# Two edits to a scheduled decoder-layer kernel: the extra tokens' values are written into the tile of the second sweep's transposed keys, and the first norm's weight is spread over the partitions ahead of its bias

## Chip, cores and metric

The kernel runs on one core of one Trainium2 chip. The metric is device time in microseconds (us) of one launch. Matrix multiplications run on TensorE (PE in the profile; PEld is its weight load), elementwise work on VectorE (DVE), ScalarE (ACT) and GpSimd (POOL); SyncE (SP) issues all DMA transfers.

## What is computed

One layer of a hybrid decoder for 2048 prompt tokens, 16 meta tokens and 32 sample tokens of width 1024, all in float32. Every token is layer-normed and multiplied by one wide input projection. Half of the result feeds a chunkwise linear recurrence (mLSTM, 4 heads of 128, chunks of 128 tokens), the other half a sliding-window attention (8 query heads, 2 key/value heads, window 128, a learned sink per head). Both halves are gated, joined, projected, added to the residual and layer-normed again.

```python
hp = layer_norm(concat([meta, x_prompt]), ln0_g, ln0_b)
hs = layer_norm(x_sample, ln0_g, ln0_b)
mq, mk, mv, mo, mz, mi, mf, aq, ak, av, az = split_proj(hp @ w_in[l] + b_in[l])
h_m, (c1, n1, m1) = mlstm_prompt(*mlstm_inputs(mq, mk, mv, mi, mf))   # chunk after chunk
h_a = swa_prompt(q_a, k_a, v_a, sink)                                  # banded blocks of 128
hp = layer_norm(DN_ALPHA * hp + concat([gate(h_m), gate(h_a)]) @ w_out, ln_g, ln_b)
```

The sample tokens go through the same layer with their own states and key/value caches. Outputs are both token sets, the states and the updated caches.

## The kernel before

The 2048 prompt tokens are 16 chunks of 128. The kernel goes over them twice. The **first sweep** (`a_steps`, to about 590 us) norms a chunk, projects q, k, v and the output gate of the recurrence, and runs the recurrence. The **second sweep** (`b_load` to `o_last`) does attention, gates, the output projection and the last norm. In the first sweep a generator `jobs` is advanced between the steps of the chunks; it does the 48 extra tokens' work (32 sample and 16 meta tokens), prepares the second sweep's weights and stores them.

Weights are split into two float16 parts (`prep_steps`: L259 and L261 find the largest value, L135 to L137 spread a maximum over the partitions by a product with an identity, L273 and L276 write the two parts). A product of a chunk with a weight of 512 columns is then 24 matmuls of 128x512 (L298, L299, L301). Chunk 0 doesn't wait for that: its four projections and the gates are taken from the raw float32 weights (`proj32`, L417). All projections write to two PSUM buffers of tag `pj`, so the third projection in a row needs the first one's result to have been copied out.

**The start.** The first norm's weight `gbr[:, 0:1024]` and bias `gbr[:, 1024:2048]` lie on one partition. Four matmuls with a row of ones spread them over 128 partitions: the bias at L359 into two `pt` buffers, which ACT copies to `bs` (L360); the weight at L369 into two `pj` buffers, which DVE reads directly for chunk 0 (L372, `(x - mean) * weight`, in two halves) and which ACT copies to `gs` (L375) for later chunks. L373 then multiplies by the reciprocal deviation and adds the bias. PE transposes the normed chunk (L450), ACT copies the transposes out (L451), and with that the first projection (L417) can start.

**The extra tokens' values.** `ve` is where the projected values of the 48 extra tokens stand, with a column of ones per head: 4 heads of 129 columns. It is `vaug[1]`. `vaug[0]` and `vaug[1]` are also where the values of even and odd chunks go (L430), and their columns of ones are set once. L317 writes `ve`; a DMA stores it to DRAM (`e_d`), and four small matmuls (L651) make the recurrence's first state `Cst[0]` from its meta tokens' rows. Chunk 1's values (L430) overwrite the same tile, so they stand behind both. The other extra tokens' results go the same way: L317 writes, `e_d` stores, and the first step of `d_head` (L690 and on) loads one head's part back into the tile `da`, from which PE transposes it (L699).

**What sets the order.** The text of the program is not the order of the instructions. The framework's scheduler replays the program with a cost table of its own and places each engine's instructions one by one; engines then run their lists strictly in that order and wait on semaphores. An edit in one place can therefore move instructions on all engines. Two orders are tied by hand: the first loads (`first`), and later transfers behind the load of a chunk (`Order.anchor`).

`kTs` holds the second sweep's transposed keys, 4 x 272 float16 per partition. Nothing reads or writes it in the first sweep until the meta tokens' keys are copied in (L888).

```python
ve = vaug[1][:NE]                                                     # L546
V.scalar_tensor_tensor(out, ps3, w.ev[:rows], t3, op0=ALU.mult, op1=ALU.add)   # L317, out = ve
c.v = vaug[n % 2]                                                     # L429
T.matmul(ps[:, i, :129], kwe[NS:NE, h], ve[NS:NE, h], start=True, stop=True)   # L651
```

Of the kernel before, what the change touches and what calls it, by code (L numbers as in the profile page):

```python
# [8 lines left out]
F32 = mybir.dt.float32  # L9
F16 = mybir.dt.float16  # L10
BF16 = mybir.dt.bfloat16
I32 = mybir.dt.int32
AF = mybir.ActivationFunctionType
# [3 lines left out]
P = 128  # L17
D = 1024
# [4 lines left out]
NE = NS + NM  # L23
H = 4
# [13 lines left out]
NW = 272  # L38
# [3 lines left out]
def tile_hymba_step(  # L42
# [7 lines left out]
    V, A, G, T, S = nc.vector, nc.scalar, nc.gpsimd, nc.tensor, nc.sync  # L50

    cst = ctx.enter_context(tc.tile_pool(name="cst", bufs=1))
# [6 lines left out]
    def psum(tag, shape, bufs):  # L59
        return pp.tile(shape, F32, tag=tag, name=tag, bufs=bufs)  # L60

    def pj():
        return psum("pj", [P, 512], 2)

    def pt(shape):
        return psum("pt", shape, 3)
# [4 lines left out]
    def po(shape):  # L71
        return psum("po", shape, 2)
# [8 lines left out]
    def work(tag, shape, dt=F32, bufs=None):  # L81
        return mn.tile(shape, dt, tag=tag, name=tag, bufs=bufs or KB4.get(tag, 1))
# [72 lines left out]
    ones = cst.tile([P, P], F32, name="ones")  # L155
# [16 lines left out]
    gbr = mn.tile([P, 2048], F32, tag="wkv", name="gbr")[0:1]  # L172
# [43 lines left out]
    vaug = [cst.tile([P, H, 129], F32, name=f"vaug{i}") for i in range(2)]  # L216
# [113 lines left out]
    def layer_norm_stats(x, rows, eps, tag):  # L330

        st = small(f"st_{tag}", 12)[:rows]
        for i in range(2):
            V.bn_stats(st[:, 6 * i:6 * i + 6], x[:, 512 * i:512 * i + 512])
        mv = small(f"mv_{tag}", 2)[:rows]
        V.bn_aggr(mv, st)
        ve = small(f"ve_{tag}", 1)[:rows]
        V.tensor_scalar(ve, mv[:, 1:2], eps, None, op0=ALU.add)
        rs = small(f"rs_{tag}", 1)[:rows]
        G.tensor_tensor(rs, ve, mhalf[:rows, 0:1], op=ALU.pow)  # L340
        return mv, rs
# [12 lines left out]
    V.tensor_scalar(xnorm, xnorm, 32.0, None, op0=ALU.mult)  # L354
    gs, bs = work("gb", [P, D]), work("gb", [P, D])

    for i in range(2):
        ps = pt([P, 512])
        T.matmul(ps, ones[0:1, :], gbr[:, D + 512 * i:D + 512 * i + 512], start=True, stop=True)  # L359
        A.activation(bs[:, 512 * i:512 * i + 512], ps, AF.Copy)  # L360
    bqk = cst.tile([P, 2], F32, name="bqk")
    all_max(bqk, bq2)

    def ln0_first(x):

        mv, rs = layer_norm_stats(x, P, EPS, "a")
        pg = [pj() for _ in range(2)]
        for i in range(2):
            T.matmul(pg[i], ones[0:1, :], gbr[:, 512 * i:512 * i + 512], start=True, stop=True)  # L369
        for i in range(2):  # L370
            c = slice(512 * i, 512 * i + 512)
            V.scalar_tensor_tensor(x[:, c], x[:, c], mv[:, 0:1], pg[i], op0=ALU.subtract, op1=ALU.mult)  # L372
        last = V.scalar_tensor_tensor(x, x, rs, bs, op0=ALU.mult, op1=ALU.add)  # L373
        for i in range(2):
            A.activation(gs[:, 512 * i:512 * i + 512], pg[i], AF.Copy)  # L375
        return last.ins
# [42 lines left out]
    def a_proj(n, i, st=None):  # L419
# [11 lines left out]
        else:  # L431
# [10 lines left out]
            if i == 3:  # L442
                A.activation(t, t, AF.Tanh, scale=0.5)

    ln0_first(x0)
    xf = [work(t, [P, 4, P]) for t in ("wt", "SI")]
    for i in range(2):
        ps = pt([P, 4, P])
# [94 lines left out]
    qe = work("qs", [P, 512])[:NE]  # L543
    ke = work("At", [P, 512])[:NE]
    oe = work("g", [P, 512])[:NE]
    ve = vaug[1][:NE]  # L546

    sto = stage(512, "w")
    load(sto, w_a[3])
# [14 lines left out]
    ps = pt([P, 8, NE])  # L564
# [3 lines left out]
    ps = pt([P, 8])  # L568
# [78 lines left out]
    for j in range(2):  # L647
        ps = po([P, 2, 256])
        for i in range(2):
            h = 2 * j + i  # L650
# [186 lines left out]
    mg = col(4)  # L837
    dma(mg, m_g)
    wB = {}

    kTs = cst.tile([P, 4, NW], F16, name="kTs")

    Vm = [cst.tile([P, 2, 4, 64], F16, name=f"Vm{i}") for i in range(2)]

# [673 lines left out]
```

## Time and profile before

| what | us |
|---|---|
| median of 3 runs (lowest to highest) | 1062.38 (1060.8 to 1063.92) |
| the profiled execution | 1059.23 |
| its span from the first to the last instruction | 1057.4 |
| PE busy | 1026.1 (97%) |
| DVE busy | 728.7 (69%) |
| ACT busy | 441.3 (42%) |
| POOL busy | 247.6 (23%) |
| mean granted TensorE clock | 0.993 |

The profile is one execution. A row of the timeline gives start and length in us, engine, source line, operation, the tile written and the tiles read, and in brackets how long the engine had been idle and what ended that. A row of the waits gives who waited for whom, the total, the number of times and the longest. A row of the windows gives busy time per engine in a stretch, then the granted clock. A row's numbers are taken from this execution, so that sums are made against 1059.23 us, of which 1.83 us lie around the span.

### The profile page before, as it was taken

Reading aid. Unit: us, or ns where it says so; the run is one execution under the profiler, and the core shown is the slowest. Engines: PE = TensorE matmul, PEld = TensorE weight load, DVE = VectorE, ACT = ScalarE, POOL = GpSimd, SP = SyncE. Lnnn points to the kernel's source line nnn. Section 1 sums busy time; section 2 is a strip of 40 time slices with the busy share of each in tenths; the row PEclk is TensorE's granted clock in tenths of the full one; section 3 lists DMA queues with packets and bytes.
Section 4 is the critical chain, followed back from the end, with each engine's and each line's share of the span. In section 5 each row is a group of like instructions: output and inputs, shape, how many; then the busy total and the mean of one; then the engine's idle time right before and its main releaser. Section 6 shows DMA issues by size and latency. Waiting matters only on the chain.

```text
span 1057.4 us, 17650 instructions
## 1 busy us (share of the span) xinstructions
PE 1026.1 (97%) x6399; PEld 571.0 (54%) x6399; DVE 728.7 (69%) x2056; ACT 441.3 (42%) x1112; POOL 247.6 (23%) x270
## 2 busy tenths in 40 slices
PE   7998999999999999999999999999999999999996
PEld 3544666655556555555565555555555455555552
DVE  5996876767766887787557676656566566666674
ACT  5783333336244554552334334343334333343430
POOL 2101313211111001013111332233331233332322
PEclk9998999999999999999999999999999999999998
DMA  9946366464794775755866463555445555545452
GB/s 332 267 133 164 99 145 154 115 187 88 233 236 123 222 247 140 231 133 160 291 188 124 92 160 89 132 131 117 108 113 127 128 124 139 108 102 135 113 114 76
DMA packets 245809, 161.83 MB, mean 153 GB/s; under 512 B 207945, under 2 KB 220953, under 8 KB 244409
## 3 DMA queue, kind: packets, MB, share of 16 engines
q1 hardware_dynamic: 245722, 160.70, 58.3%
q8 instruction: 50, 0.82, 0.3%
q14 instruction: 37, 0.30, 0.1%
HBM read 68.22 MB, written 43.58 MB: 106 GB/s over the span
## 4 chain that ended last, share of the span: by engine, by line
PE 69%; DMA 11%; DVE 10%; ACT 6%; issue 3%; POOL 1%; SPq 1%; DVEq 0%; ACTq 0%
PE pj L1351 14%; PE pj L301 14%; PE pj L298 14%; PE pj L299 14%; DMA stg<-hl 3%; PE pt L1271 3%; PE po L1324 2%; DMA stg<-in_dram 1%; DMA xT<-hl 1%; DMA kT<-kh 1%; ACT w_o L259 1%; DMA wd_o<-w_o 1%; DVE w_o L276 1%; PE po L816 1%; PE po L817 1%
## 5 line engine op out<-in xcount | busy, mean ns | idle before, releaser
L301 PEld LDWEIGHTS <-xT 128*128 128x128 f16 x992 | 96.9, 98 | 98.2 <-issue 1.0
L299 PEld LDWEIGHTS <-xT 128*128 128x128 f16 x992 | 97.4, 98 | 96.7 <-issue 5.2
L298 PEld LDWEIGHTS <-xT 128*128 128x128 f16 x992 | 97.4, 98 | 94.1 <-issue 2.8
L1351 PEld LDWEIGHTS <-EE 128*128 128x128 f16 x720 | 70.3, 98 | 79.0
L1351 PE MATMUL pj<-wr_o,EE 128*128 128x512 f16 x360 | 82.3, 379 | 0.0
L1351 PE MATMUL pj<-w_o,EE 128*128 128x512 f16 x360 | 82.1, 379 | 0.0
L1278 ACT ACTIVATE SI<-SI,nb 128x272 f32<-128x272 f32 (+1 forms) x64 | 32.4, 507 | 66.0 <-DVE nb L1275 66.0
L298 PE MATMUL pj<-w_o,xT 128*128 128x512 f16 x120 | 46.9, 390 | 3.2 <-DVE vaug L430 3.2
L1278 ACT ACTIVATE g<-g,nb 128x272 f32<-128x272 f32 (+1 forms) x64 | 32.2, 503 | 42.4 <-DVE nb L1275 42.4
L1284 POOL TENSOR_TENSOR mhl<-SI,mhl 128x32 f16<-128x32 f32 x32 | 12.6, 395 | 157.6 <-ACT mhl L1283 157.6
L298 PE MATMUL pj<-wr_az,xT 128*128 128x512 f16 x128 | 48.5, 379 | 0.0
L299 PE MATMUL pj<-wr_z,xT 128*128 128x512 f16 x128 | 48.5, 379 | 0.0
L298 PE MATMUL pj<-wr_aq,xT 128*128 128x512 f16 x128 | 48.5, 379 | 0.0
L299 PE MATMUL pj<-wr_aq,xT 128*128 128x512 f16 x128 | 48.5, 379 | 0.0
L299 PE MATMUL pj<-wr_az,xT 128*128 128x512 f16 x128 | 48.5, 379 | 0.0
L298 PE MATMUL pj<-wr_z,xT 128*128 128x512 f16 x128 | 48.5, 379 | 0.0
L793 POOL TENSOR_TENSOR qs<-qs,SI 128x512 f32<-128x512 f32 x16 | 20.9, 1307 | 113.5 <-ACT SI L784 113.3
L299 PE MATMUL pj<-w_o,xT 128*128 128x512 f16 x120 | 46.7, 390 | 0.0
L1181 POOL TENSOR_TENSOR xs<-xs,gb 128x1024 f32<-128x1024 f32 (+1 forms) x16 | 42.8, 2674 | 15.4 <-DMA stg<-hl 9.3
L298 PE MATMUL pj<-w_v,xT 128*128 128x512 f16 x120 | 46.0, 383 | 0.0
L299 PE MATMUL pj<-w_v,xT 128*128 128x512 f16 x120 | 45.8, 382 | 0.0
L792 POOL TENSOR_TENSOR qs<-qT 128x512 f32<-128x512 f16 x16 | 20.2, 1260 | 109.2 <-DMA qT<-qh 58.9
(463 smaller groups left out, 2492.1 us busy)
## 6 DMA issues: line engine op xcount, KB each, us to landing
stg<-in_dram SPq DMA_DIRECT2D x28, 512.0 KB
xs<-in_dram SPq DMA_DIRECT2D x16, 512.0 KB
h_d<-xs SPq DMA_DIRECT2D x16, 512.0 KB
xT_d<-xT SPq DMA_DIRECT2D x16, 512.0 KB
xs<-h_d SPq DMA_DIRECT2D x16, 512.0 KB
xT<-xT_d SPq DMA_DIRECT2D x16, 512.0 KB
out_dram<-xs SPq DMA_DIRECT2D x15, 512.0 KB
hn_d<-g SPq DMA_DIRECT2D x16, 258.0 KB
```

Of the source, the lines that this page charges most:

```text
L259: A.activation(w.t[:, 2 * i:2 * i + 2, 0, :], s, AF.Abs, accum_out=mx4[:, i:i + 1])
L298: T.matmul(ps, xT[:, k, :], w.t[:, k, 0, :n], start=(k == 0), stop=False)
L299: T.matmul(ps, xT[:, k, :], w.t[:, k, 1, :n], start=False, stop=False)
L301: T.matmul(ps, xT[:, KT + k, :], w.t[:, k, 0, :n], start=False, stop=(k == KT - 1))
L792: G.tensor_tensor(c.qs, c.qT[:, 0], c.qT[:, 1], op=ALU.add)
L793: G.tensor_tensor(c.qs, c.qs, c.SI, op=ALU.mult)
L1181: G.tensor_tensor(z, z, lg[:rows], op=ALU.mult)
L1271: T.matmul(ps[:, lo:], c.qT[:, h], kTs[:, 2 * (h // 4) + x, lo:], start=(x == 0), stop=(x == 1))
L1278: A.activation(p[:, i, lo:], p[:, i, lo:], AF.Exp, bias=nb[:, h:h + 1], accum_out=sums[:, h:h + 1])
L1284: G.tensor_tensor(m[:, 1], p[:, :, 2 * P:], m[:, 0], op=ALU.subtract)
L1324: T.matmul(pso[:, h], l, r, start=False, stop=(i == len(last) - 1), skip_group_check=True)
L1351: T.matmul(ps, c.yT[:, a, :], w[:, k, t, :], start=(first and j == 0), stop=(last and j == len(mm) - 1))
```

## The change

```diff
@@ -354,10 +354,6 @@
     gs, bs = work("gb", [P, D]), work("gb", [P, D])
 
-    for i in range(2):
-        ps = pt([P, 512])
-        T.matmul(ps, ones[0:1, :], gbr[:, D + 512 * i:D + 512 * i + 512], start=True, stop=True)
-        A.activation(bs[:, 512 * i:512 * i + 512], ps, AF.Copy)
     bqk = cst.tile([P, 2], F32, name="bqk")
     all_max(bqk, bq2)
 
@@ -367,6 +363,10 @@
         pg = [pj() for _ in range(2)]
         for i in range(2):
             T.matmul(pg[i], ones[0:1, :], gbr[:, 512 * i:512 * i + 512], start=True, stop=True)
+        for i in range(2):
+            ps = pt([P, 512])
+            T.matmul(ps, ones[0:1, :], gbr[:, D + 512 * i:D + 512 * i + 512], start=True, stop=True)
+            A.activation(bs[:, 512 * i:512 * i + 512], ps, AF.Copy)
         for i in range(2):
             c = slice(512 * i, 512 * i + 512)
             V.scalar_tensor_tensor(x[:, c], x[:, c], mv[:, 0:1], pg[i], op0=ALU.subtract, op1=ALU.mult)
@@ -543,7 +543,11 @@
-    ve = vaug[1][:NE]
+
+    kTs = cst.tile([P, 4, NW], F16, name="kTs")
+
+    ve = kTs.rearrange("p c t -> p (c t)").bitcast(F32)[:NE, 0:H * 129].rearrange("p (h d) -> p h d", d=129)
+    G.memset(ve[:, :, P:P + 1], 1.0)
@@ -838,8 +842,6 @@
-    kTs = cst.tile([P, 4, NW], F16, name="kTs")
-
```

The first edit writes the two bias matmuls and their copies behind the two weight matmuls. The second puts `ve` into the memory of `kTs`, seen as float32 (516 of its 544 words), so that `vaug[1]` belongs to odd chunks alone; a small memset sets the four columns of ones. No arithmetic is added or removed but that memset. The new file has the weight's matmuls at L365, the bias's at L368 and its copies at L369. From the third hunk on, a line of the new file is that of the old plus 4, and from the fourth on plus 2.

The scheduler makes another order of the whole first sweep from it; in the second sweep the order is the same again, from about 590 us on. Three places follow.

On DVE at the start, before, L373 (the norm's last step; `xs` is chunk 0, `gb` the bias) stands close behind the second L372. L137 and L135 are the two ends of a maximum that is spread through PE:

```order
L372 SCALAR_TENSOR_TENSOR xs<-xs,mv_a,pj 128x512
L261 TENSOR_REDUCE mx_268<-stg 128x1
L261 TENSOR_REDUCE mx_414<-tg 128x1 x3
L372 SCALAR_TENSOR_TENSOR xs<-xs,mv_a,pj 128x512
L598 MEMSET ea 128x8
L261 TENSOR_REDUCE mx_414<-tg 128x1
L135 TENSOR_SCALAR dg<-cs,gb_187 128x128
L373 SCALAR_TENSOR_TENSOR xs<-xs,rs_a,gb 128x1024
L265 TENSOR_REDUCE mx<-mx_268 128x1
L265 TENSOR_REDUCE mx<-mx_414 128x1
L137 TENSOR_REDUCE gbx<-po 128x2
L135 TENSOR_SCALAR dg<-cs,gb_198 128x128
```

And now, the last rows up to L373:

```order
L353 TENSOR_TENSOR cols<-gbx 128x1
L122 TENSOR_SCALAR cols<-cols 128x1
L354 TENSOR_SCALAR cols<-cols 128x1
L124 TENSOR_SCALAR cols<-cols 128x1
L265 TENSOR_REDUCE mx<-mx_270 128x1
L126 TENSOR_SCALAR cols<-cols 128x1
L265 TENSOR_REDUCE mx<-mx_416 128x1
L135 TENSOR_SCALAR dg<-cs,gb_198 128x128
L261 TENSOR_REDUCE mx_490<-stage 128x1
L137 TENSOR_REDUCE bqk<-po 128x2
L135 TENSOR_SCALAR dg<-cs,mx 128x128
L373 SCALAR_TENSOR_TENSOR xs<-xs,rs_a,gb 128x1024
```

Both L372 now stand ahead of L261, and L373 stands behind two whole spread maxima (`gbx`, `bqk`) and one reduction of a weight. PE's list has the L136 matmuls of these maxima ahead of the transposes L450 in the same way.

On ACT at the start, before (`gb<-pt` is a half of the bias, `gb<-pj` one of the weight, `wt` and `SI` hold chunk 0's transposes):

```order
L360 ACTIVATE gb<-pt 128x512 x2
L259 ACTIVATE w_q,mx_268<-stg 128x2x512 x3
L375 ACTIVATE gb<-pj 128x512
L323 ACTIVATE hl,lns<-xs 48x1024
L375 ACTIVATE gb<-pj 128x512
L259 ACTIVATE w_k,mx_488<-stage 128x2x512
L324 ACTIVATE lns<-lns 48x1
L451 ACTIVATE wt<-pt 128x512
```

And now:

```order
L369 ACTIVATE gb<-pt 128x512
L375 ACTIVATE gb<-pj 128x512 x2
L259 ACTIVATE w_q,mx_270<-stg 128x2x512 x3
L323 ACTIVATE hl,lns<-xs 48x1024
L369 ACTIVATE gb<-pt 128x512
L259 ACTIVATE w_k,mx_490<-stage 128x2x512
L324 ACTIVATE lns<-lns 48x1
L259 ACTIVATE w_k,mx_490<-stage 128x2x512
L325 ACTIVATE hl,lns<-xs,lns 48x1024
L620 ACTIVATE hl<-xs,cols 128x1024
L326 ACTIVATE lns<-lns,cols 48x1
L451 ACTIVATE wt<-pt 128x512
```

The second half of the bias has moved behind four long instructions, and the copy of the transposes (L451) behind four more.

On DVE where chunk 1's values are copied out (L430, `vaug_125` is `vaug[1]`), before; `mx_1803<-stg` reads the freshly loaded k/v weight of the second sweep, `da` the sample tokens' states, and `g<-px` is the last of the extra tokens' four projections:

```order
L696 COPY da<-ea 128x8
L614 COPY ea<-pt 48x12
L644 TENSOR_SCALAR kw<-At,ea 48x128 x4
L696 COPY da<-ea 128x8
L261 TENSOR_REDUCE mx_1803<-stg 128x1 x2
L311 TENSOR_TENSOR g<-g,bias 48x512
L261 TENSOR_REDUCE mx_1803<-stg 128x1
L317 SCALAR_TENSOR_TENSOR g<-px,cols,g 48x512
L430 SCALAR_TENSOR_TENSOR vaug_125<-pj,cols,bias 128x4x128
```

And now:

```order
L700 COPY da<-ea 128x8
L317 SCALAR_TENSOR_TENSOR kTs<-px,cols,g 48x4x128
L700 COPY da<-ea 128x8
L518 SCALAR_TENSOR_TENSOR gts<-pt,cols,bg 128x8
L809 SCALAR_TENSOR_TENSOR At<-pt,cols,wt 128x512
L261 TENSOR_REDUCE mx_1804<-stg 128x1
L519 SCALAR_TENSOR_TENSOR gts<-pt,cols,gts 128x8
L261 TENSOR_REDUCE mx_1804<-stg 128x1 x2
L472 SCALAR_TENSOR_TENSOR ls<-gts 128x4
L484 COPY Gi_123<-gts 128x4
L430 SCALAR_TENSOR_TENSOR vaug_125<-pj,cols,bias 128x4x128
```

L430 stands behind the same loads' readers (L700, L261) as before; L317 of the last projection (`g<-px`) has moved behind it. On PE, chunk 1's output gate projection stood behind the gates' matmuls before (`pj_1099`; `pt_847` are the gates):

```order
L516 MATMUL pt_847<-w_g_413,xT_616 128x8
L298 LDWEIGHTS xT_616
L298 MATMUL pj_1099<-w_o_620,xT_616 128x512
L299 LDWEIGHTS xT_616
L299 MATMUL pj_1099<-w_o_620,xT_616 128x512
```

And now it stands behind chunk 0's eight matmuls of L820 and L821 (L816 and L817 of the old file), which stood after it:

```order
L820 MATMUL po_922<-vaug0_124,At_799 128x129
L821 MATMUL po_922<-Cst0_673,qs_773 128x129
L820 MATMUL po_929<-vaug0_124,At_799 128x129
L821 MATMUL po_929<-Cst0_673,qs_773 128x129
L820 MATMUL po_929<-vaug0_124,At_799 128x129
L821 MATMUL po_929<-Cst0_673,qs_773 128x129
L298 LDWEIGHTS xT_618
L298 MATMUL pj_1100<-w_o_622,xT_618 128x512
```

## Prediction, made before the changed kernel was run

> **What bounds the kernel now.** I began with the page's totals (busy time, share of the span, count) and the granted clock, a digit of tenths for each of 40 slices:
>
> ```profile
> span 1057.4 us, 17650 instructions
> PE 1026.1 (97%) x6399; PEld 571.0 (54%) x6399; DVE 728.7 (69%) x2056; ACT 441.3 (42%) x1112; POOL 247.6 (23%) x270
> PEclk9998999999999999999999999999999999999998
> ```
>
> PE is busy for 97% of the span, so the time is PE's work plus PE's waits. The edits add no matmul; they can only move waits and the stretches at a lower clock. The waits of PE, by what ended them (total, times, longest):
>
> ```profile
> PE pt L359 <- DVE dg L135: 6.3, 1, 6.3
> ...
> PE pj L298 <- DVE vaug L430: 3.2, 1, 3.2
> PE pt L749 <- DVE Gf L483: 2.9, 2, 1.7
> PE pt L513 <- ACT am L773: 1.8, 1, 1.8
> PE po L136 <- DVE dg L135: 1.1, 2, 0.7
> PE pt L612 <- ACT ea L607: 1.1, 1, 1.1
> ```
>
> The row to see is L298's: 3.2 us for `vaug`, the very tile that the second edit separates from the extra tokens. The first row is the load of the first operands and stays. Then the stretches (length, busy time and count of PE, PEld, DVE, ACT and POOL, granted clock, DMA share, GB/s):
>
> ```profile
> 20.00:70.00 50.00, 50.00 (x196) 24.24 (x195) 45.79 (x125) 40.06 (x68) 7.08 (x6) 1.00 0.86 251
> 89.40:96.20 6.80, 4.43 (x11) 1.57 (x11) 5.92 (x21) 2.77 (x8) 1.27 (x1) 0.50 0.44 68
> 95.00:590.00 495.00, 487.40 (x3040) 283.05 (x3039) 358.27 (x1045) 206.29 (x495) 89.82 (x88) 1.00 0.63 172
> 396.60:400.00 3.40, 3.40 (x10) 1.17 (x9) 3.30 (x8) 3.40 (x11) 1.54 (x1) 0.50 0.30 111
> ```
>
> From 20 to 70 us PE has no gap: whatever delays its start by a microsecond delays the end by one. After 3.2 us idle the clock stood at 0.50 from 89.4 to 96.2, and once more at 396.6.
>
> **The start.** Timeline of before, first PE, then DVE and ACT:
>
> ```profile
> 6.26 3.75 PE L359 MATMUL pt<-gbr,ones 1*128 1x512 f32 x4 [6.26 <-DVE dg L135]
> 9.80 3.62 PE L369 MATMUL pj<-gbr,ones 1*128 1x512 f32 x4
> 14.88 0.79 PE L136 MATMUL po<-dg,ones 128*128 128x128 f32 x2 [0.74 <-DVE dg L135]
> 16.08 1.97 PE L450 MATMUL pt<-cs,xs 128*128 128x128 f32 x8 [0.40 <-DVE xs L373]
> 19.43 4.45 PE L417 MATMUL pj<-stg,wt 128*128 128x512 f32 x8
> 23.72 3.60 PE L417 MATMUL pj<-stage,wt 128*128 128x512 f32 x8
> ...
> 13.81 0.74 DVE L372 SCALAR_TENSOR_TENSOR xs<-xs,mv_a,pj 128x512 f32<-128x512 f32 x1
> 14.55 0.28 DVE L135 TENSOR_SCALAR dg<-cs,gb 128x128 f32<-128x128 f32 x1
> 14.74 1.28 DVE L373 SCALAR_TENSOR_TENSOR xs<-xs,rs_a,gb 128x1024 f32<-128x1024 f32 x1
> 16.07 0.41 DVE L137 TENSOR_REDUCE gbx<-po 128x2 f32<-128x256 f32 x1
> 17.04 1.21 DVE L261 TENSOR_REDUCE mx<-stage 128x1 f32<-128x1024 f32 x1
> ...
> 10.04 0.60 ACT L360 ACTIVATE gb<-pt 128x512 f32<-128x512 f32 x1 [1.11 <-PE pt L359]
> 12.61 1.04 ACT L259 ACTIVATE w_q<-stg 128x1024 f16<-128x1024 f32 x1
> 14.13 1.05 ACT L323 ACTIVATE hl<-xs 48x1024 bf16<-48x1024 f32 x1
> 17.27 0.57 ACT L451 ACTIVATE wt<-pt 128x512 f32<-128x512 f32 x1
> 17.75 1.14 ACT L616 ACTIVATE hl<-xs,cols 128x1024 f16<-128x1024 f32 x1
> ```
>
> The four spreading matmuls change places at equal cost, 3.75 against 3.62 us; each half is out 1.7 to 1.9 us after the one before. The weight's are now out at about 8.2 and 9.9, the bias's at 11.7 and 13.4. So L372 can run some 3.5 us earlier, but the chunk's norm ends with L373, which needs the bias, and that now comes last.
>
> ACT: first bias half at 11.7, two weight copies to 13.4 (0.6 each), three L259 at 1.04 to 16.5, L323 to 17.6, the second bias half to 18.1. In before the second half was there at 10.6. L323 and the L259 read other data, so nothing lets the copy past them: ACT's list is strict.
>
> DVE: the second L372 is no longer what L373 stands behind; it stands behind two spread maxima, each a round trip to PE. From a first L135 at 13.8, a trip takes about 1.2 us until L137 can start (14.55 to 16.07 here with L373 between; 1.2 without); L137, the next L135, seven tiny rows (0.6 together), one L261 (1.2), the second L137 (0.4) and L135 end at about 18.4. Both paths meet at 18.1 to 18.4, so L373 starts at 18.4, not 14.74: 3.7 later. L450 follows at 19.7. L451 stands on ACT behind two L259, L325, L620 (1.14, the old L616) and L326 from 18.1 on, to about 22.7, while the transposes are there at about 21; so ACT, not PE, sets L417's start: 22.7 and L451's 0.6 make 23.3 against 19.43, **+3.9**. Two pairs of L136 that stood later now run in that hole: −0.46 (0.23 a pair at full clock, as 0.38 us with overlap in a full stretch). Net **+3.4**.
>
> The clock at the start: the first eight rows of L417 took 4.45 us, the next eight 3.60, so 0.85 us were lost because PE began at the low rate, and the spreading matmuls ran low too (L369's four rows of 512 columns took 3.62 us, as long as L417's second eight). With a longer hole ahead of L417, PE may run low for one more window of about 3.4 us (half of 89.4 to 96.2): half of that is the most, 1.7. The new hole's own waste counts already, so 0 to 1.5; I take **+0.9**, the amount seen.
>
> Here the Trainium skill (TensorE: Matmul & The Clock Gate, Part 1: The HAM clock gate) says that one busy window of about 3.4 us raises the clock and one idle window lowers it. The trace disagrees at this place: PE was busy from 6.26 to 13.4 and L417 still began slowly. By the page the first matmuls would lift the clock in either order; by it the term is 0 and the sum 0.9 lower.
>
> **Around 90 us.** Rows of PE, DVE, ACT and SP:
>
> ```profile
> 80.35 0.29 PE L612 MATMUL pt<-cs,ea 128*48 128x128 f32 x1 [1.10 <-ACT ea L607]
> 91.77 0.58 PE L298 MATMUL pj<-w_o,xT 128*128 128x512 f16 x1 [3.19 <-DVE vaug L430]
> 99.23 0.31 PE L699 MATMUL px<-cs,da 32*128 32x32 f32 x2
> 104.44 0.39 PE L817 MATMUL po<-Cst,qs 128*128 128x129 f32 x2
> 73.59 3.65 DVE L276 SCALAR_TENSOR_TENSOR w_o<-stage,cols,w_o 128x1024 f16<-128x1024 f32 x3
> 85.54 0.17 DVE L696 COPY da<-ea 128x8 f32<-128x8 f32 x1 [1.53 <-DMA da<-in_dram]
> 87.72 1.50 DVE L261 TENSOR_REDUCE mx<-stg 128x1 f32<-128x512 f32 x2 [2.00 <-DMA stg<-in_dram]
> 90.33 0.73 DVE L317 SCALAR_TENSOR_TENSOR g<-px,cols,g 48x512 f32<-48x512 f32 x1
> 90.99 0.73 DVE L430 SCALAR_TENSOR_TENSOR vaug<-pj,cols,bias 128x512 f32<-128x512 f32 x1
> 96.45 0.31 ACT L706 ACTIVATE da<-da 32x128 f32<-32x128 f32 x1 [1.23 <-DMA da<-e_d]
> ```
>
> L430 was late not because of L651's reading: DVE had no idle time before it. It stood behind rows that waited for transfers (1.53 and 2.00 us). These transfers are issued when the preparation of `w_o` ends (77.2), and L430 ends 14.5 us after that. The separate tile alone gives nothing; the new order must. There, that end comes at about 78.3 (1.1 us more of DVE's rows ahead of it, counted from the list), and L430, with L317 of `g` behind it, ends 13.4 after: 91.7. PE arrives at `w_o` at 88.6 + 3.4 + 0.9 − 1.4 (L612, below) + 1.8 (eight matmuls L820/L821 now ahead, 0.22 each: starts 104.21 and 104.44) = 93.3. So PE no longer waits, with 1.6 us to spare: **−3.2** and, for the slow stretch behind it (PE's 4.43 us of it would take half at full clock), **−2.2**. The eight moved matmuls cost nothing in sum.
>
> L612's gap (1.1 and 0.3 for its queue) is filled since its rows stand earlier on all engines: **−1.4**, at worst 0.
>
> New: `g` now stands behind L430, with one L261, L433, L438, L311 and its own L317 (0.7 each) and nine tiny rows of about 0.15 from there on, 4.7 in all: it ends at about 96.4. From its end (91.06) to the first reader of the reloaded `da` (96.45) it took 5.4, so `da` is there at 101.8, while PE reaches L703 (the old L699; behind 24 matmuls of `w_o` at 0.216 and some 1.9 us of small ones, 7.1 in all) at 100.4: **+1.4 to 1.6**, here 1.6.
>
> The rest of the first sweep is in a new order too; its waits (L749 2.9, L513 1.8, four small ones 1.4, and 1.7 for the slow stretch at 396.6) make 7.8. I see no side for it: 0, bounds −7.8 to +7.8. The memset on POOL (23% busy) and the `kTs` tile, unused until the sweep's end, cost nothing; if POOL were late, L430 no longer reads that column, only L655 does.
>
> **Sum:** 3.4 + 0.9 − 1.4 − 3.2 − 2.2 + 1.6 = **−0.9**: 1059.23 − 0.9 = 1058.3 for such an execution. The median of the runs lies 3.15 above the profiled time, so 1061.5 against 1062.38.
>
> **Rivals.** *Faster (A):* half of the 7.8 us of small waits go with the new order on top: −3.9 more, −4.8, 1057.6. For it: each hangs on one row's place (L749 on `Gf`). Against: new orders make new waits.
>
> *Slower (B):* PE still waits for `vaug` L430, because its place on DVE behind the same transfers is unchanged. If the preparation of `w_o` ends 1.6 us later than 78.3 (half of the start's delay handed on), the wait begins; 3.2 later again, all of it is there. Then 3.2 + 2.2 stay; the wait at L703 falls to 1.2: −0.9 + 5.4 − 0.4 = +4.1, 1066.4. DVE was busy for 45.8 of 50 us from 20 to 70, so it has little room to catch up; that speaks for it.
>
> *Clock (C):* the new wait at L703 costs a slow window as the 1.8 us wait at L513 did at 396.6: +1.7, 1063.2. The Trainium skill's rule of a whole idle window (same section) speaks against it; the row at 396.6, where 1.8 us sufficed, for it.
>
> *The edit does not do what it says:* as found, freeing the tile gives nothing by itself; that is B's ground.
>
> **How the numbers follow.** Forecast −0.9: 0.38; C: 0.10; A: 0.30; B: 0.22. A measurement of this kernel tells about 0.3%, 3.2 us, from no change, so faster is below 1059.2, slower above 1065.6: A 0.30, B 0.22, the rest 0.48. Range: A with 2 us more to B with 0.6 more, 1055.5 to 1067.0; the bounds of the reordered rest beyond that are left out. The likeliest case alone spans 1059.5 to 1063.5 (start's clock 0 to 1.5, L612's gap kept).
>
> **What would show it.** L373 at about 18.4 and L417 at 23.3; no row of L298 waiting for `vaug`, and the clock at 1.00 from 80 to 96; a wait of 1 to 2 us at L703 for `da`; L749 and L513 still waiting about 5 us together. A start of L417 below 20 or a wait of 3 us for L430 would make the sum wrong; equal steps and a time off by over 4 us would mean the rest of the first sweep decided.

## The result, and the profile after

The changed kernel is slower: 1070.44 us median of 3 runs (1069.25 to 1071.47) against 1062.38, ratio 1.0055 [1.0031, 1.008]. Timed again with 12 runs against 29 of before it took 1069.57 against 1064.25, 1.0050 [1.0032, 1.0068]. The forecast was 1061.5, range 1055.5 to 1067.0.

The head of the page after, with busy time, share and count per engine:

```profile
span 1068.6 us, 17656 instructions
PE 1029.2 (96%) x6399; PEld 572.2 (54%) x6399; DVE 729.5 (68%) x2056; ACT 441.5 (41%) x1112; POOL 251.9 (24%) x271
```

PE's busy time grew by 3.1 us of 11.2, at the same number of matmuls; the rest are gaps. The waits of PE, by what ended them (total, times, longest):

```profile
PE po L1326 <- DMA stg<-hl: 6.2, 7, 2.8
...
PE px L738 <- DVE ea L722: 3.0, 2, 1.9
...
PE po L655 <- DVE kTs L317: 1.8, 1, 1.8
...
PE px L703 <- DMA da<-e_d: 1.4, 1, 1.4
```

No row of L298 waits for `vaug` and none of L616 (the old L612) for ACT. In their place stand L655, which reads `ve` out of `kTs`, and L738, a step of the sample tokens. The stretches that the prediction showed, and one that is new:

```profile
20.00:70.00 50.00, 49.66 (x189) 25.26 (x189) 45.01 (x125) 39.22 (x68) 5.54 (x5) 1.00 0.87 239
89.40:96.20 6.80, 6.80 (x41) 4.12 (x39) 6.55 (x17) 2.92 (x8) 1.15 (x1) 1.00 0.45 107
182.90:186.30 3.40, 3.40 (x10) 1.22 (x8) 3.40 (x12) 0.46 (x2) 0.12 (x1) 0.50 0.47 124
```

The granted clock (the number behind POOL's busy time) is 1.00 where it was 0.50 from 89.4 to 96.2, and 0.50 at 182.9.

Single waits don't add up to the difference, so PE's loss is counted for every matmul: the time to the next matmul's start, less what a matmul of that shape takes at full clock (the 25% quantile of the shape in the profiles of before and after). The loss holds gaps and low clock together; only the time ahead of about 6 us and the tail lie outside it. Two single runs far off, 1531 us of e1 and 2758 us of e6, are in no ratio. By stretch of the span, in us, with all runs (a ratio is the estimate on record, with its 95% interval, against before's runs on the same chip, and differs from the ratio of the two medians by up to 0.0011; "before" is the profile of the prediction):

| kernel | ratio [95%] | span | L417 starts | 0–40 | 40–70 | 70–130 | 130–240 | 240–480 | 480–600 | 600– |
|---|---|---|---|---|---|---|---|---|---|---|
| before | 1 | 1057.4 | 19.43 | 6.0 | 0.3 | 9.6 | 5.8 | 11.7 | 4.5 | 4.0 |
| b0_before | a single run | 1065.9 | 19.86 | 7.7 | 0.5 | 10.0 | 5.6 | 13.2 | 9.3 | 4.2 |
| f3_before_10 | 0.9976 [0.9956, 0.9996] | 1058.4 | 19.14 | 5.3 | 0.3 | 9.3 | 5.5 | 12.1 | 6.6 | 4.4 |
| after | 1.0055 [1.0031, 1.008] | 1068.6 | 23.04 | 10.0 | 0.2 | 5.5 | 10.7 | 12.1 | 6.7 | 7.8 |
| a0_after | 1.0050 [1.0032, 1.0068] | 1070.7 | 22.57 | 9.6 | 0.2 | 6.3 | 12.5 | 10.9 | 7.9 | 8.2 |
| f1_after_10 | 1.0031 [1.001, 1.0052] | 1061.0 | 22.28 | 10.6 | 0.2 | 5.0 | 8.4 | 12.3 | 4.7 | 5.4 |
| f2_after_24 | 1.0071 [1.0043, 1.0098] | 1070.9 | 22.13 | 9.7 | 0.3 | 5.5 | 10.6 | 15.0 | 6.7 | 8.9 |
| e1_bias_only | 1.0047 [1.0028, 1.0066] | 1070.8 | 22.89 | 9.6 | 0.2 | 6.8 | 8.9 | 12.1 | 9.5 | 8.3 |
| e2_ve_only | 1.0075 [1.0051, 1.0099] | 1071.5 | 19.20 | 7.0 | 0.5 | 10.1 | 6.6 | 17.3 | 6.5 | 8.8 |
| e4_tie | 1.0028 [1.0007, 1.0049] | 1065.5 | 22.71 | 10.5 | 0.2 | 6.4 | 7.0 | 13.2 | 5.2 | 7.9 |
| e6_decay8 | 1.0015 [0.9996, 1.0034] | 1062.9 | 23.22 | 9.0 | 0.2 | 6.1 | 5.7 | 11.6 | 7.0 | 7.5 |
| e5_start | 1.0101 [1.0077, 1.0126] | 1074.7 | 20.81 | 9.8 | 0.5 | 11.6 | 7.2 | 19.8 | 3.9 | 7.4 |
| e7_kv_behind | 1.0094 [1.0067, 1.0121] | 1071.8 | 19.26 | 7.0 | 0.5 | 11.9 | 7.8 | 18.2 | 5.8 | 5.8 |
| e8_short_start | 1.0134 [1.0099, 1.017] | 1073.9 | 18.74 | 8.0 | 1.1 | 14.8 | 9.2 | 11.1 | 5.8 | 9.2 |
| e9_both | 1.0129 [1.0098, 1.016] | 1075.5 | 19.23 | 7.7 | 1.5 | 18.4 | 6.5 | 11.1 | 6.3 | 8.8 |
| e10_final_dve | 0.9959 [0.9936, 0.9982] | 1053.8 | 19.81 | 6.9 | 0.4 | 9.5 | 6.3 | 9.8 | 1.9 | 4.2 |
| e11_o_dve | 0.9968 [0.9947, 0.9989] | 1057.7 | 19.53 | 6.2 | 0.5 | 9.4 | 5.6 | 13.2 | 1.4 | 5.8 |

The means of after, a0 and e1 (the same lists but for two swaps on DVE), less those of before and b0: +2.9, −0.2, −3.6, +5.0, −0.8, +1.1, +4.0, in all +8.4, as much as the mean spans differ. The ratio of the runs, 1.0050 of 1064.25, gives +5.3: a profile is one execution, and with 1.83 us around the span before's two lie 0.8 below their median, the other three some 2 above theirs.

### The profile page after: what moved, and what is told of

Its sections match the earlier page's. It is cut to its first block, busy times and chain, and to the rows that moved or that the text cites. A ratio compares the mean times of both kernels' runs of the same rounds, so it can differ in the third digit from the quotient of the medians.

```text
span 1068.6 us, 17656 instructions
## 1 busy us (share of the span) xinstructions
PE 1029.2 (96%) x6399; PEld 572.2 (54%) x6399; DVE 729.5 (68%) x2056; ACT 441.5 (41%) x1112; POOL 251.9 (24%) x271
## 4 chain that ended last, share of the span: by engine, by line
PE 55%; DMA 18%; DVE 13%; issue 6%; ACT 5%; POOL 2%; SPq 1%; DVEq 0%; ACTq 0%; POOLq 0%
PE pj L1353 13%; PE pj L301 11%; PE pj L299 11%; PE pj L298 11%; DMA stg<-hl 4%; DMA xT<-hl 2%; PE pt L1273 2%; PE po L1326 2%; DVE xs L382 2%; DMA stg<-in_dram 1%; DMA wd_o<-w_o 1%; DMA wd_z<-w_z 1%; DMA wt<-hn_d 1%; DMA da<-e_d 1%; ACT w_o L259 1%
## 5 line engine op out<-in xcount | busy, mean ns | idle before, releaser
L298 PEld LDWEIGHTS <-xT 128*128 128x128 f16 x992 | 97.5, 98 | 93.2 <-issue 2.9
L299 PEld LDWEIGHTS <-xT 128*128 128x128 f16 x992 | 97.4, 98 | 93.1 <-issue 2.5
L327 POOL TENSOR_TENSOR lns<-lns,mhalf 128x1 f32<-128x1 f32 (+1 forms) x16 | 19.8, 1238 | 135.0 <-ACT lns L326 135.0
L298 PE MATMUL pj<-wr_az,xT 128*128 128x512 f16 x128 | 48.5, 379 | 0.0
L298 PE MATMUL pj<-wr_aq,xT 128*128 128x512 f16 x128 | 48.5, 379 | 0.0
L299 PE MATMUL pj<-wr_aq,xT 128*128 128x512 f16 x128 | 48.5, 379 | 0.0
L299 PE MATMUL pj<-wr_az,xT 128*128 128x512 f16 x128 | 48.5, 379 | 0.0
L298 PE MATMUL pj<-wr_z,xT 128*128 128x512 f16 x128 | 48.5, 379 | 0.0
L299 PE MATMUL pj<-wr_z,xT 128*128 128x512 f16 x128 | 48.5, 379 | 0.0
L298 PE MATMUL pj<-w_o,xT 128*128 128x512 f16 x120 | 46.2, 385 | 0.3 <-DVE k L433 0.3
L299 PE MATMUL pj<-w_k,xT 128*128 128x512 f16 x120 | 46.5, 388 | 0.0
L298 PE MATMUL pj<-w_k,xT 128*128 128x512 f16 x120 | 46.5, 387 | 0.0
L299 PE MATMUL pj<-w_o,xT 128*128 128x512 f16 x120 | 46.4, 387 | 0.0
```

Of the source, the lines that this page charges most:

```text
L298: T.matmul(ps, xT[:, k, :], w.t[:, k, 0, :n], start=(k == 0), stop=False)
L299: T.matmul(ps, xT[:, k, :], w.t[:, k, 1, :n], start=False, stop=False)
```

## The experiments

**The change again.** No edit.

> The changed kernel once more, for its interval on the same chip as the next three. Theory (the first edit makes the order and the order makes the time): 7 to 9 us above the kernel before, L417 at about 23, waits of PE for L722 at L738 of about 3 us and a stretch at half clock after the longest, as in the first look. Rival (much of the 11 us between the two profiles is the spread of single executions): 2 to 4 us above before, and the stretches at half clock elsewhere or missing.

1.0050, and the table's row: the slowdown and its places repeat, though at 5.3 us it is less than the 7 to 9 expected.

**Each edit alone.** e1 keeps `ve = vaug[1][:NE]` and `kTs` in their old places; e2 keeps the bias ahead of the weight.

> The first edit alone. Its orders on PE, ACT and SP are those of the changed kernel. Theory (the second edit does nothing once the first is made): within 1 us of the changed kernel, L417 at 23, the waits at L738 in the same places. Rival (the second edit costs by itself, by the tile in the memory of the keys or by its memset): 3 us or more faster than the changed kernel. A further rival (the second edit does free PE from a wait for vaug): slower than the changed kernel by 3 to 5 us, with a wait of L298 for vaug.

> The second edit alone. Its start is that of before, and L430 of chunk 1 now stands ahead of the rows that wait for transfers, and every L722 ahead of the L382 behind which it stands in the changed kernel. Theory: L417 at 19.4, no wait of L298 for vaug and full clock from 80 to 96 (3.2 and 2.2 us less), no wait at L738: 4 to 6 us faster than before, give or take 3 for the small waits of a new order. Rival (the second edit's new order costs what the changed kernel lost after 120 us): 2 to 5 us slower than before.

e1 is as slow as the whole change (1.0047). Its lists on PE, ACT and SP are those of after; on DVE two neighbouring pairs are swapped. So beside the first edit the second adds nothing that the runs can tell. e2 alone was to be 4 to 6 us faster and is 1.0075. L417 starts at 19.20, as before, and the wait for `vaug` is gone: L430 now starts at 80.58, ten microseconds sooner than in before.

```profile
80.58 0.73 DVE L430 SCALAR_TENSOR_TENSOR vaug<-pj,cols,bias 128x512 f32<-128x512 f32 x1
```

Yet from 70 to 130 us PE loses 10.1 against 9.6 to 10.0, and from 240 to 480 it loses 17.3. Its waits of PE:

```profile
PE pt L807 <- DMA kT<-kh: 3.7, 1, 3.7
PE pt L753 <- DVE g L822: 2.5, 1, 2.5
PE px L703 <- DMA da<-e_d: 2.5, 1, 2.5
PE pt L772 <- DVE rM L763: 2.3, 1, 2.3
PE px L738 <- DVE da L739: 2.0, 1, 2.0
```

All five are waits of the new order, at other places than after's. The clock is at half at 121, 268, 503 and 1046 us.

**Before once more, and the norm step that delays L738.** b0 is before without an edit. e4 puts the last step of three chunk norms (L382) behind the `ea` of the head (L722) that it had overtaken:

```diff
-        V.scalar_tensor_tensor(x, x, rs, bs[:rows], op0=ALU.mult, op1=ALU.add)
+        with tc.issue_after(Order.e[h]):          # h = 1, 2, 3 in the sixth to eighth norm
+            V.scalar_tensor_tensor(x, x, rs, bs[:rows], op0=ALU.mult, op1=ALU.add)
```

> The kernel before, profiled a second time, since its first profile (1059.23 us) lies at the low end of its 29 runs (median 1064.25). Theory (the waits repeat, and what differs between executions is which of them drop the clock, and the transfers of the second sweep): the waits of L298 for vaug (3.2 us), L749 and L513 in the same places within 0.5 us each, and 2 to 5 us more at other stretches of half clock. Rival (the low profile was another order of events in the first sweep): the wait at L298 differs by over 1 us.

> The changed kernel, with three L382 (those of the sixth to eighth norm) tied behind the L722 that stood behind them. The order is the same up to about 120 us and new after that. Theory (L382 ahead of L722 makes the waits at L738): the three waits (about 4 us) and the half clock behind the second (1.7) go, so 4 to 6 us faster than the changed kernel. Rival (the waits only move on, since the later L382 makes the chunk's transposed tokens late): within 2 us of it, with waits of L298 or L301 for xT in their place.

b0 has a span of 1065.9, 8.5 longer than before's first profile with the same lists: 1.7 of it up to 40 us, 1.5 from 240 to 480 and 4.8 from 480 to 600, where L749's wait for `Gf` is 3.0 instead of 1.7 us and the clock stands at half from 498 and from 573 us. So two profiles of one kernel can differ by more than the edit's 5.3 us. The place to look at is after's, near 178 us, first POOL, then DVE and PE (start and length; the bracket holds idle time and what ended it):

```profile
178.30 1.92 POOL L732 TENSOR_TENSOR da<-da,ea 128x1032 f32<-128x1032 f32 x1
...
176.64 1.28 DVE L381 SCALAR_TENSOR_TENSOR xs<-xs,lns,gb 128x1024 f32<-128x1024 f32 x1 [1.58 <-ACT hl L325]
178.37 2.93 DVE L382 SCALAR_TENSOR_TENSOR xs<-xs,lns,gb 128x1024 f32<-128x1024 f32 x1 [0.44 <-POOL lns L327]
181.29 0.27 DVE L722 SCALAR_TENSOR_TENSOR ea<-da,px 32x128 f32<-32x128 f32 x1
...
181.70 0.90 PE L738 MATMUL px<-da 32*128 32x129 f32 x6 [1.94 <-DVE ea L722]
```

The same step in before (L718 is L722, L728 is L732, L734 is L738):

```profile
176.72 1.91 POOL L728 TENSOR_TENSOR da<-da,ea 128x1032 f32<-128x1032 f32 x1
...
176.32 0.27 DVE L718 SCALAR_TENSOR_TENSOR ea<-da,px 32x128 f32<-32x128 f32 x1
176.78 2.93 DVE L382 SCALAR_TENSOR_TENSOR xs<-xs,lns,gb 128x1024 f32<-128x1024 f32 x1 [0.19 <-POOL lns L327]
177.72 0.93 PE L734 MATMUL px<-da 32*128 32x129 f32 x6
```

L382 takes 2.93 us where L381 with the same shape takes 1.28. In before that hurts nobody, since the short row that PE needs stands ahead of it; in after it stands behind, PE waits, and the clock falls to half. With the tie (lines 8 higher: L746 is L738, L761 is L753, L521 is L513) the loss from 130 to 240 falls from 12.5 in a0 to 7.0, and the time to 1.0028, 2.9 us less in the median where 4 to 6 were expected. Not all of the 5.5 arrives, as other waits grow:

```profile
PE px L746 <- POOL lns L329: 0.6, 1, 0.6
...
PE pt L761 <- DVE Gf L491: 3.3, 2, 2.4
PE pt L521 <- ACT am L785: 2.7, 1, 2.7
```

**Is it GpSimd's L732 that stretches L382?** e6 leaves the order alone and cuts that row to an eighth:

```diff
-        G.tensor_tensor(C3, C3, dec.unsqueeze(2).to_broadcast([P, 8, 129]), op=ALU.mult)
+        G.tensor_tensor(C3[:, 0:1], C3[:, 0:1], dec[:, 0:1].unsqueeze(2).to_broadcast([P, 1, 129]), op=ALU.mult)
```

> The changed kernel, with GpSimd's L732 cut to one of its eight states, so that the decay of the other seven is left out. The orders on PE, DVE, ACT and SP are those of the changed kernel. Theory (L382 takes 2.9 instead of 1.28 us because L732, 1.92 us on GpSimd, runs beside it, and that is most of the wait at L738): L382 at 1.3 us in all places, the waits at L738 fall from 4.0 to 0.5 us or less and the half clock behind the second goes, so 3 to 5 us faster than the changed kernel (a ratio to before near 1.001). Rival (L382 is long for another reason, such as its own operands): L382 still at 2.9 us, the time within 1 us of the changed kernel.

```profile
177.14 1.41 DVE L382 SCALAR_TENSOR_TENSOR xs<-xs,lns,gb 128x1024 f32<-128x1024 f32 x1 [0.44 <-POOL lns L327]
178.54 0.27 DVE L722 SCALAR_TENSOR_TENSOR ea<-da,px 32x128 f32<-32x128 f32 x1
178.96 0.90 PE L738 MATMUL px<-da 32*128 32x129 f32 x6 [0.40 <-DVE ea L722]
```

With unchanged lists L382 falls to 1.41 and PE's wait from 1.94 to 0.40; the loss from 130 to 240 is 5.7, before's own size, and the time 1.0015 [0.9996, 1.0034]. In after L382 ends 1.08 us (its own length, nearly) behind the end of L732 at 180.22. It looks as if it stood still meanwhile. The Trainium skill (SBUF — State Buffer, Who interferes with whom) says so: a VectorE instruction with two SBUF inputs and a GpSimd instruction that reads SBUF exclude each other from a shared pair of ports, and the second to issue waits until the first is done. The trace agrees, here and in e10 (below), where L476 ends at 489.84 beside a GpSimd row that ends at 489.83.

**The start, shorter by order.** e5 is after with the spread of `bqk` held behind L373, and with the copies of the weight and the preparation of `w_q` held behind the second copy of the bias:

```diff
-    all_max(bqk, bq2)
...
-    ln0_first(x0)
+    with tc.issue_after(ln0_first(x0)):
+        all_max(bqk, bq2)
...
+    with tc.issue_after(Order.bias):
+        wA[0] = prep("q", stq, 512, sums=(0, 1, 2))
```

> Both edits, with the start tied: the weight copies and the reductions of w_q on ACT behind the second bias copy, and the second spread maximum on DVE behind L373. DVE has L373 in its old place, and the PE order of the last 4464 of 5956 matmul rows is that of the second edit alone. Theory (the order sets the waits): L417 at about 19, no wait for vaug, and the second edit's later waits in the same places (L807 for the transposed keys 3 to 4 us near 263, L772 near 395, L753 near 500), so within 2 us of the second edit alone, 6 to 9 us slower than before. Rival (those waits were the luck of transfers): L807 does not wait, 3 us or more faster than the second edit alone.

L417 starts at 20.81, 1.8 to 2.2 sooner than after's but not at 19, and the time is 1.0101. The wait that the rival counted on is nearly absent (L810 is L807), but others stand in its stead (L775, L706 and L619 are L772, L703 and L616):

```profile
PE pt L775 <- DVE rM L766: 3.3, 3, 2.6
PE px L706 <- DMA da<-e_d: 2.9, 2, 2.1
PE pt L619 <- DVE ea L611: 2.0, 1, 2.0
...
PE pt L810 <- DMA kT<-kh: 0.2, 1, 0.2
```

Neither theory had these: the tie made another order of everything behind it, and from 240 to 480 us PE loses 19.8.

**The wait for `vaug` by order alone.** e7 is before, the shared tile kept, with the k/v weight's reductions (L261) tied behind chunk 1's L430:

```diff
+                if name == "kv" and Order.v1 is not None:
+                    with tc.issue_after(Order.v1):
+                        V.tensor_reduce(mx4[:, i:i + 1], ...)
```

> The kernel before, with nothing but the four L261 of the key/value weight tied behind chunk 1's L430. Theory (L430 was late because it stood behind the readers of that transfer): no wait of L298 for vaug, full clock from 89 to 96, 5.4 us less there; what the new order behind it gives back isn't known, 0 to 8 us, so 1058 to 1067. Rival (L430 was late for L651's reading of the shared tile, which the second edit removes): a wait of 2 us or more of L298 for vaug remains.

DVE and PE (L436 is L430, L304 is L298):

```profile
89.33 0.75 DVE L436 SCALAR_TENSOR_TENSOR vaug<-pj,cols,bias 128x512 f32<-128x512 f32 x1 [2.63 <-DMA e_d<-vaug]
```

```profile
PE pj L304 <- DVE vaug L436: 1.9, 1, 1.9
```

Freed of the rows ahead of it, L430 waits for the store of `ve` out of the shared tile, 2.63 us, and PE still waits for it. So the shared tile is a second lock behind the first. The kernel is slower as a whole, 1.0094.

**The start, shorter by less work.** e8 is after with the maximum of `w_q` and `w_k` (L259) taken over 64 of 512 columns, e9 the same on top of e6:

```diff
-                A.activation(w.t[:, 2 * i:2 * i + 2, 0, :], s, AF.Abs, accum_out=mx4[:, i:i + 1])
+                c = slice(0, 64 if name in ("q", "k") else n)
+                A.activation(w.t[:, 2 * i:2 * i + 2, 0, c], s[:, :, c], AF.Abs, accum_out=mx4[:, i:i + 1])
```

> The changed kernel, with ACT's L259 of w_q and w_k cut to an eighth of their columns, so that the search for those two weights' largest values leaves out the rest. That takes about 4 us from ACT's list ahead of L451, and L373 now stands ahead of the second spread maximum. The order from 120 us on is that of the changed kernel. Theory (ACT's list at the start costs 3 us of the total): L417 at 20 or earlier, instead of 22 to 23, and 2.5 to 4 us faster than the changed kernel (ratio to before near 1.002). Rival (the time gained at the start is lost again near 85, where L655 waits for L317 behind a transfer): the wait of L655 grows by 2 us or more, within 1.5 us of the changed kernel.

> The last kernel with GpSimd's L732 cut to one of eight states as well, so that it leaves out both the rest of those two searches and the decay of seven states. Orders on PE, DVE, ACT and SP are those of the last kernel. Theory (start and blocked L382 are two separate terms that add): 3 to 4 us faster than the last, 6 to 8 us faster than the changed kernel, within 2 us of before. Rival (they overlap): within 1.5 us of the better of the two alone.

L417 starts at 18.74 (L418 in this file), 3.8 sooner than in a0, and the kernel is slower than a0, 1.0134 against 1.0050. Its waits of PE, and then DVE's rows (L299, L434, L262 are L298, L433, L261):

```profile
PE pj L299 <- DVE k L434: 3.6, 2, 3.3
```

```profile
91.27 2.78 DVE L262 TENSOR_REDUCE mx<-stg 128x1 f32<-128x512 f32 x4 [1.78 <-DMA stg<-in_dram]
...
99.10 0.73 DVE L434 SCALAR_TENSOR_TENSOR k<-pj,cols,bias 128x512 f32<-128x512 f32 x1
```

The start's gain is lost again between 70 and 130 us (14.8 against 6.3): `k` of the next chunk stands behind reductions that wait for a load. e9 loses even more there, 18.4, and its cut from 130 to 240 (6.5) doesn't show in the time. So neither run prices the start by itself, since the list behind it was not the same.

**The same pair of engines elsewhere.** In b0, at 490 us, POOL and DVE:

```profile
490.62 2.35 POOL L1181 TENSOR_TENSOR xs<-xs,gb 32x1024 f32<-32x1024 f32 x1 [1.52 <-DVE ls L474]
493.04 2.35 POOL L1182 TENSOR_TENSOR xs<-xs,gb 32x1024 f32<-32x1024 f32 x1
...
491.20 0.15 DVE L475 RECIPROCAL ls<-ls 128x4 f32<-128x4 f32 x1
491.39 1.60 DVE L476 TENSOR_TENSOR ls<-ls 128x4 f32<-128x4 f32 x1
493.22 2.20 DVE L478 TENSOR_SCALAR ls<-ls 128x4 f32<-128x4 f32 x1
```

Rows of four words take 1.60 and 2.20 us and end when GpSimd's rows do (492.99 and 492.97; 495.42 and 495.39), while L475, with one input, takes 0.15 beside them. e10 is before with the extra tokens' last two norm steps on DVE; e11 adds that the first o weight's maxima go to DVE instead of ACT, so that L513 need not wait for ACT:

```diff
-        G.tensor_tensor(z, z, lg[:rows], op=ALU.mult)
-        G.tensor_tensor(z, z, lb[:rows], op=ALU.add)
+        e = V if rows < P else G
+        e.tensor_tensor(z, z, lg[:rows], op=ALU.mult)
+        e.tensor_tensor(z, z, lb[:rows], op=ALU.add)
...
-        yield from prep_steps(w, f"o{i}", ahead[f"o{i}"], 512, mg=mg, sums=range(4))
+        yield from prep_steps(w, f"o{i}", ahead[f"o{i}"], 512, mg=mg, sums=() if i == 0 else range(4))
```

> The kernel before, with the two products of the extra tokens' last norm (L1181 and L1182, 2.35 us each on GpSimd near 491) on DVE. The order differs only from about 490 to 600 us. Theory (L476 and L478, which take 1.6 and 2.2 us there instead of 0.16, wait for those two on GpSimd): L476 and L478 back at 0.2 us, the wait of L749 for Gf at 495 falls from 3.0 to 1.5 us or less, and 1 to 3 us faster than before. Rival (DVE's two added rows of 1.2 us make Gf as late): the wait stays at 2.5 us or more, no change.

> The last kernel (before, with the extra tokens' last norm on DVE), and the four reductions of the first half of the output weight moved from ACT's L259 to DVE's L261. L259 writes the tile that the transfer wd_z still reads, and ACT's L773 stood behind the four; L261 writes no such tile. The order differs from the last kernel's from about 370 to 440 us only. Theory (L513's wait for am near 393, 1.8 to 2.7 us, and the half clock behind it are ACT's queue): that wait goes, 2 to 4 us faster than the last kernel, a ratio to before near 0.993. Rival (the four reductions of 1.2 us each now stand ahead of other rows on DVE, idle there for 4.7 us, and a wait for DVE takes the place): within 1 us of the last kernel, ratio near 0.996.

e10 is faster than both kernels: 1059.75 us, 0.9959 [0.9936, 0.9982]. Its lists differ from before's only between about 490 and 600 us, and there the loss is 1.9 (before, b0 and f3: 4.5, 9.3, 6.6). L476 falls from 1.60 to 1.11 us (it still meets another GpSimd row, L792, which runs from 487.66 to 489.83), L478 from 2.20 to 0.17, and the longest wait of L749 for `Gf` to 0.8 (before 1.7, b0 3.0). Since f3, a build with before's lists, reached 0.9976 (below), the edit's own worth is read from that stretch rather than from the ratio: 2.6 us against before's profile, which has no half clock there.

```profile
488.73 1.11 DVE L476 TENSOR_TENSOR ls<-ls 128x4 f32<-128x4 f32 x1
490.42 0.17 DVE L478 TENSOR_SCALAR ls<-ls 128x4 f32<-128x4 f32 x1
```

e11 has the same small loss there (1.4) and is no better (0.9968 [0.9947, 0.9989]). The wait of L513 for ACT is gone, and PE waits for DVE's copy of another projection instead, as the rival had it:

```profile
PE pj L298 <- DVE o L433: 2.4, 1, 2.4
```

**The second sweep, and how much a build scatters.** After's order loses 4 us more than before's behind 600 us, although the lists there are the same. One place is L1326's wait near 696 us. To see whether it hangs on when the engines load their code, f1, f2 and f3 put instructions that do nothing at the start (10, 24, and 10 in before), which shifts the code and leaves the lists alone:

```diff
+    for _ in range(10):
+        V.memset(nul[0], 0.0)
+        G.memset(nul[1], 0.0)
+        A.activation(nul[2], ones[:, 0:1], AF.Copy)
```

> The changed kernel with ten one-column fills each on DVE and GpSimd and ten one-column copies on ACT at the start, which nothing reads; all orders stay. Theory (code loads that fall on a transfer's last part make L1326 wait): the code loads of those three engines come ten instructions earlier, the sixteenth part lands with the others, and the wait of 1.1 us at the L1326 near 696 goes; the total may win 1 to 3 us or lose them again where another load now falls. Rival (the late part comes from the order of the transfers on SP): the wait of 1.0 to 1.2 us stays.

> The same with 24 of each. Theory: the wait near 696 gone again, or back if another code load falls there; whenever it is there, a code load of GpSimd, ACT or DVE starts within the 0.5 us ahead of the transfer's landing. Rival: the wait of 1.0 to 1.2 us stays whatever the code loads do.

> The kernel before with ten of each. All orders stay. Theory: within 3 us of before, up or down; a wait of over 1 us at the L1324 near 690 only if a second code load starts within 0.5 us ahead of the landing. Rival: no change of any wait in the second sweep by over 0.3 us.

The theory fell: L1326's wait stays in f1 and f2, at 1.15 us. In f2 one load of code starts ahead of the landing (697.96) and a part lands late (699.95); in f3 two do (688.78 and 688.95) and none is late. What the three runs showed instead is the scatter. f1 and f2, timed on one chip with the same lists, lie 4.9 us (0.4%) apart in the median, and f3 is 0.24% [0.04, 0.44] below before, with no work changed but the fillers. All builds of after's order (1.0031 to 1.0071) still lie above both of before's (1 and 0.9976), so the change's sign stands; a difference of 0.2 to 0.4% between two single builds does not.

## Why the prediction was wrong

**The start: right.** L373 was forecast at 18.4 and L417 at 23.3. PE, DVE and ACT after:

```profile
23.04 5.09 PE L417 MATMUL pj<-stg,wt 128*128 128x512 f32 x8
...
17.78 1.22 DVE L261 TENSOR_REDUCE mx<-stage 128x1 f32<-128x1024 f32 x1 [0.61 <-DMA stage<-in_dram]
19.44 1.28 DVE L373 SCALAR_TENSOR_TENSOR xs<-xs,rs_a,gb 128x1024 f32<-128x1024 f32 x1
...
21.19 1.13 ACT L620 ACTIVATE hl<-xs,cols 128x1024 f16<-128x1024 f32 x1
22.41 0.57 ACT L451 ACTIVATE wt<-pt 128x512 f32<-128x512 f32 x1
```

L373 came a microsecond later, of which 0.61 was L261's wait for its load; L451 behind L620 on ACT sets L417, as the text said, so that this second did not add. L417's first eight rows took 5.09 instead of 4.45: +0.6 where +0.9 was put. In all +4.3 was forecast up to 40 us; the first two profiles differ by 4.0, the means by 2.9.

**Around 90 us: right in what goes, short in what comes.** L612's gap and the wait for `vaug` are gone in all profiles of the new order, and L703 waits 1.4 (forecast 1.4 to 1.6). The slow stretch is gone in after, but a0 has half clock from 89.6 to 93.0, behind a wait of 2.17 at L655. Not foreseen was L655:

```profile
87.11 0.15 DVE L700 COPY da<-ea 128x8 f32<-128x8 f32 x1
87.18 0.73 DVE L317 SCALAR_TENSOR_TENSOR kTs<-px,cols,g 48x512 f32<-48x512 f32 x1
...
87.97 1.16 PE L655 MATMUL po<-kTs,kw 16*128 16x129 f32 x8 [1.80 <-DVE kTs L317]
```

In DVE's list in the section on the change, L317 of `ve` stands behind the first L700, which reads a transferred tile; the text followed L430 down that list and not L317. The terms made −5.2 here; the means give −3.6.

**The step that failed: "The rest of the first sweep is in a new order too … I see no side for it: 0, bounds −7.8 to +7.8."** From 130 to 600 us it was +5.3 in the means, +5.0 of it between 130 and 240, where L382 overtook L722 three times: after's L738 waits 3.6 us there in all, and the half clock behind the longest wait adds 1.7. The order showed that, and before's trace had the price in it: an L382 of 2.93 us beside L728 (L732 of the new file). e6 and e4 show the cause from two sides. The bounds held the 5.3, but the range was drawn without them. That the steps before it came nearly as forecast and the time was off by 8.9 is what the text itself named as the sign that the rest of the first sweep decided.

**A second step, left out altogether:** behind 600 us, where the lists are the same, after's profiles lose 4.0 us more. Four places make most of it: L1326 waits 1.1 us near 696 and 0.5 near 859, where no profile of before's lists waits, its last wait is 2.8 instead of 2.1, and the half clock behind that, from 1043, costs some 1.6 us (a0, e1 and f2 have it too). In e2, whose start is before's, and in f2 the loss there is 8.8 and 8.9; in f1, without that half clock, 5.4. At 688 us in before and 695 in after, a stretch of two microseconds round the same matmuls:

```profile
688.30:690.30 2.00, 2.00 (x53) 1.67 (x51) 1.56 (x4) 1.36 (x5) 1.78 (x1) 1.00 0.01 5
```

```profile
695.25:697.25 2.00, 0.87 (x27) 0.75 (x25) 1.12 (x3) 1.35 (x5) 1.79 (x1) 1.00 0.03 9
```

In after one of the 16 parts of the transfer `stg<-hl` lands at 697.17, the one before it at 695.61 (before: 688.80 and 688.62), with the DMA engines idle (share 0.03). Why that part is late stays open. It comes with the order of the first sweep: L1326's wait there, 1.0 to 1.3 us, is in all twelve profiles whose first sweep has another order than before's, and in none of the five that keep before's up to 380 us (before, b0, f3, e10, e11).

**The base.** The sum was put on a profiled execution of 1059.23, at the low end of before: 29 runs gave 1059.17 to 1069.83, median 1064.25. That bears on the forecast time, not on its sign.

**The rivals.** B had the sign and about the size (+4.1 against +5.3 by the runs), not the mechanism: L430 isn't waited for. A's small waits went in part, without a gain: L749 (L753 in the new file) waits nowhere in after, and L836 waits 4.0 in all instead, where L832 in before waited 0.6; from 240 to 600 us the loss changes by 0.3. C's price fell due elsewhere in after (182.9), but in e1, with nearly the same lists, at L703's own place: 1.82 us of waiting, then half clock from 103.5 to 106.9. "Freeing the tile gives nothing by itself" holds as far as the first edit stands beside it (e1); alone, in e2, the wait did go, and e7 shows that without the free tile L430 would meet the store of `ve` next.

**The sum again, by means:** +2.9 up to 40 us, −0.2 and −3.6 up to 130, +5.3 up to 600, +4.0 behind. What the prediction worked out comes to −0.9, as it said, though both its halves were 1.4 to 1.6 too large and that cancelled, which is luck; what it put at zero or left out decided.

## What to carry to other kernels

When an edit lets a scheduler make a new order, price the whole new list and not the place that the edit meant: look for each long row that has overtaken a short one for which PE waits, above all a long DVE row that runs beside GpSimd. Six orders newly made here over most of the first sweep (the change, e2, e4, e5, e7, e8) were all slower than before's, by 0.3 to 1.3%, while an edit that moved rows only between 490 and 600 us (e10) came out 0.4% faster, a size that fillers alone nearly reach. Before a difference of 0.2 to 0.4% is given to an edit, time a second build with the same lists.

## What the runs showed of the hardware

- DVE rows that began while a GpSimd row ran often ended with that row or after it: 2.93 instead of 1.28 us for 128x1024, 1.60 and 2.20 us for 128x4, where 0.17 suffices. Of the DVE rows that took over 0.3 us more than the median of their line, tiles and shape, 23 of 24 in before and 20 of 21 in after began beside a running GpSimd row, and none of these ended ahead of it. Not each pair does this: an L381 at 374.23 in after took 1.26 beside a GpSimd row that ran from 374.01 to 376.51.
- Waits of PE of about 2 us sometimes halve the clock and sometimes not, with the same lists: after drops at 182.9 behind 1.94 us; f1, with waits of PE up to 2.7 us, has no half clock until 1056.5. The Trainium skill (TensorE: Matmul & The Clock Gate, Part 1: The HAM clock gate) has the windows free-running, which fits that the same wait drops the clock or not; that a whole idle window is needed does not fit, as 1.94 us was enough. The traces show where the difference lies: within a profile all changes of the clock lie whole steps of 3.413 us apart (before: 21.14, 89.41, 96.23, 396.60; after: 25.88, 182.89, 186.30, 500.33). Over the 17 profiles, every step at full clock in which PE had 2.0 us or more without a matmul was followed by half clock (36 of 36); with 1.6 to 2.0 us it was 10 of 23, with less 7 of 5036. So a wait drops the clock when enough of it falls into one step: before's last L1324 wait left 1.84 us in one and dropped nothing, after's left 2.76 at the same place and did.
- Instructions that do nothing, put at the start, moved the time: 10 and 24 of them (f1, f2) lie 0.4% apart, and 10 in before (f3) gave 0.24% less.
